# Softmax times values: two rows of probabilities in one 4-byte word, values stationary over 512 columns

## The chip, the cores and the metric

One core of a Trainium2 chip. The metric is the device time of one execution in microseconds (us), median of several. A profile's span is some 1.8 us shorter than the time of the same execution (1088.4 against 1090.23 us before), because it goes from the first to the last instruction. A profile shows one execution, so a time read off a trace is that of one execution too.

## The reference

```python
# scores: (8, 12, 1024, 1024) fp32, v: (8, 12, 1024, 64) fp32
attn = np.exp(scores - scores_max)
attn = attn / (np.sum(attn, axis=-1, keepdims=True) + 1e-8)
return np.matmul(attn, v)
```

There are 96 heads. For each, 4 MiB of scores and 256 KiB of values come in and 256 KiB go out. Both kernels leave out the maximum (the scores are standard normal) and get the row sum from a column of ones beside the values (M = 65).

## The kernel before

A partition holds 8 rows of scores (R = 8). ACT makes two rows of fp16 probabilities at a time, PE transposes each row in eight blocks of 128 x 128, DVE copies the eight blocks out of PSUM, and eight accumulating products have the transposed probabilities stationary and 65 columns of values moving.

```python
# abridged
s_pool = ...(name="spool", bufs=AHEAD)          # AHEAD = 4 heads of scores
p_pool: bufs=6; pt_pool: bufs=5; psT_pool: bufs=5 (PSUM); psO_pool: bufs=3 (PSUM)
# ... cut
def finish(u):                                   # two rows behind the transposes
    n, r, pt, st = u
    # ... cut
    for c in range(C):
        nc.tensor.matmul(out=psO[:, g, :], lhsT=pt[:, c * P : (c + 1) * P],
                         rhs=st["vones"][:, c, :], start=(c == 0), stop=(c == C - 1))
    if g == G - 1:                               # every four rows
        nc.vector.reciprocal(out=recip[:], in_=psO[:, :, D : D + 1])
        nc.vector.tensor_tensor(...)             # divide into out_sb
    if r == R - 1:
        queue(nc.sync.dma_start(out=out_bh[n], in_=st["out_sb"][:]))
# ... cut
def load(n):
    queue(nc.sync.dma_start(out=v_sb[:], in_=v_bh[n]))
    step = EB if n == BH - 1 else R              # only the last head comes in pieces of two rows
    for r in range(0, R, step):
        queue(nc.sync.dma_start(out=s_nat[:, r : r + step, :], in_=sc_bh[n, :, r : r + step, :]))
# ... cut
for r in range(R):
    if r % EB == 0:
        nc.scalar.activation(out=p_nat[:], in_=s_nat[:, r : r + EB, :], func=EXP)
    for c in range(C):
        nc.tensor.transpose(out=psT[:, c * P : (c + 1) * P], in_=p_row[:, c, :], identity=ident16[:])
    nc.vector.tensor_copy(out=pt[:], in_=psT[:])
    if r == R - 1 and n + AHEAD < BH:
        load(n + AHEAD)
    # ... cut: finish() of the row two before
```

`queue` keeps all loads and stores in program order on one queue.

The softmax here doesn't subtract the row's maximum and nothing guards it: scores larger than these inputs give would overflow.

## Time and profile before

| | before |
|---|---|
| time, median (range) | 1089.68 us (1089.3 to 1089.68, 3 runs) |
| span | 1088.4 us |
| busy: PE, DVE, ACT | 72%, 58%, 65% |
| DMA queue of loads and stores | 98.5% of 16 engines, 453.00 MB |

The queue part of the page (packets, MB, share of the 16 engines): the fetches of the program's own instructions travel over the same DMA engines.

```profile
q8 instruction: 96, 1.57, 0.6%
```

The second is the granted clock, in windows of 4 us behind the landing of the last-but-one head (length, then busy us of PE, weight loads, DVE, ACT, POOL, then PEclk, DMA share, GB/s):

```profile
1066.00:1070.00 4.00, 2.02 (x18) 1.90 (x19) 1.50 (x4) 3.98 (x3) 0.62 (x1) 0.50 0.73 294
...
1074.00:1078.00 4.00, 4.00 (x88) 4.00 (x86) 3.64 (x7) 4.00 (x3) 0.00 (x0) 1.00 0.42 165
```

The mean granted clock of 0.813 is thus no steady limit but a mixture: here 0.50 behind an idle stretch of PE (3.44 us, until 1067.98), 0.64 from 1070 to 1074, and 1.00 from 1074, when PE had been busy for some 6 us.

### The profile page before, as it was taken

The page shows a single profiled execution, that of the slowest core. Times are in us where ns is not written, and L with a number is a line of the kernel's source. Part 1 is how long each engine was busy: PE and PEld are TensorE (multiplying, and loading weights), DVE is VectorE, ACT ScalarE, POOL GpSimd, SP SyncE. Part 2 cuts the span into 40 slices and gives each one's busy share as a digit, 9 for nine tenths or more (in the row PEclk, how much of TensorE's full clock was granted, in tenths as well). Part 3 has the DMA queues.
Part 4 walks back from the last instruction along what each step waited for, and adds up shares of the span by engine and source line. Part 5 has one row for each costly group of instructions (what it writes and reads, how often), then busy time and mean ns, then how long its engine had stood idle before and what let it go on. Part 6 is the DMA issues. An engine that isn't in the chain of part 4 may idle for free.

```text
span 1088.4 us, 27687 instructions
## 1 busy us (share of the span) xinstructions
PE 782.8 (72%) x12288; PEld 743.7 (68%) x12288; DVE 628.2 (58%) x1156; ACT 704.0 (65%) x385; POOL 60.1 (6%) x102
## 2 busy tenths in 40 slices
PE   3767777676777767677776767777676777767676
PEld 3667667676766767677676767677676767767676
DVE  2556556565555655556565655655565565556555
ACT  4667576666757666665766666575665757566675
POOL 0000000000000000000000000000000000000000
PEclk9888878778787877878888887878888787787888
DMA  9999999999999999999999999999999999999994
GB/s 396 423 430 425 423 423 427 427 426 428 427 422 423 424 431 427 422 426 424 431 425 429 425 426 424 425 429 428 424 423 430 424 426 427 428 420 428 426 398 160
DMA packets 42024, 454.77 MB, mean 418 GB/s; under 512 B 4656, under 2 KB 4656, under 8 KB 29232
## 3 DMA queue, kind: packets, MB, share of 16 engines
q1 hardware_dynamic: 41904, 453.00, 98.5%
q8 instruction: 96, 1.57, 0.6%
q14 instruction: 24, 0.20, 0.0%
HBM read 427.82 MB, written 25.17 MB: 416 GB/s over the span
## 4 chain that ended last, share of the span: by engine, by line
DMA 96%; DVE 1%; PE 1%; issue 0%; SPq 0%; ACT 0%; DVEq 0%; ACTq 0%
DMA out_dram<-out_sb 69%; DMA s_nat<-in_scores_dram 18%; DMA v_sb<-in_v_dram 9%; DVE out_sb L89 1%; PE psT L140 1%; PE psO L77 0%; SPq L120 0%; ACT p_nat L136 0%; DVE pt L146 0%; SPq L115 0%; DVE recip L88 0%; DVEq L89 0%; SPq L96 0%; ACTq L136 0%
## 5 line engine op out<-in xcount | busy, mean ns | idle before, releaser
L136 ACT ACTIVATE p_nat<-s_nat 128x2048 f16<-128x2048 f32 x384 | 702.8, 1901 | 375.8 <-DMA s_nat<-in_scores_dram 364.7
L140 PE MATMUL psT<-ident,p_nat 128*128 128x128 f16 x6144 | 621.6, 264 | 274.5 <-ACT p_nat L136 273.5
L140 PEld LDWEIGHTS <-p_nat 128*128 128x128 f16 x6144 | 524.9, 155 | 301.5 <-ACT p_nat L136 295.2
L146 DVE COPY pt<-psT 128x1024 f16<-128x1024 f16 x768 | 529.0, 691 | 307.2 <-PE psT L140 285.4
L77 PE MATMUL psO<-vones,pt 128*128 128x65 f16 x6144 | 343.0, 204 | 27.3 <-DVE pt L146 26.3
L77 PEld LDWEIGHTS <-pt 128*128 128x128 f16 x6144 | 295.4, 107 | 39.2 <-DVE pt L146 38.3
L89 DVE TENSOR_TENSOR out_sb<-psO,recip 128x256 f32<-128x256 f32 x192 | 73.6, 420 | 98.7 <-DMA out_dram<-out_sb 98.6
L130 POOL CAST vones<-v_sb 128x512 f16<-128x512 f32 x96 | 59.4, 619 | 1007.3 <-DMA v_sb<-in_v_dram 995.5
L88 DVE RECIPROCAL recip<-psO 128x4 f32<-128x4 f32 x192 | 34.1, 178 | 49.9 <-PE psO L77 49.9
L136 ACT ACT_TABLE_LOAD x1 | 1.3, 1283 | 0.7 <-PEq L168 0.7
L64 DVE MEMSET vones<- 128x8 f16 x3 | 0.1, 65 | 0.8 <-PEq L168 0.8
L58 DVE CAST ident<-ident 128x128 f16<-128x128 f32 x1 | 0.2, 227 | 0.4 <-POOL ident masks.py:199 0.4
masks.py:199 POOL TENSOR_SCALAR_AFFINE_SELECT ident<-ident 128x128 f32<-128x128 f32 x1 | 0.3, 294 | 0.1
masks.py:197 POOL MEMSET ident<- 128x128 f32 x1 | 0.2, 205 | 0.3 <-POOLq L168 0.3
L168 POOL MEMSET const-float32-0.0<- 128x1 f32 x1 | 0.1, 99 | 0.2 <-issue 0.2
L168 POOL MEMSET const-bfloat16-1.0<- 128x1 bf16 x1 | 0.1, 102 | 0.0
L168 POOL MEMSET const-uint8-127<- 128x1 uint8 x1 | 0.1, 102 | 0.0
L168 POOL MEMSET const-float32-1.0<- 128x1 f32 x1 | 0.1, 99 | 0.0
## 6 DMA issues: line engine op xcount, KB each, us to landing
s_nat<-in_scores_dram SPq DMA_DIRECT2D x95, 4096.0 KB, 32.5
v_sb<-in_v_dram SPq DMA_DIRECT2D x96, 256.0 KB, 23.5
out_dram<-out_sb SPq DMA_DIRECT2D x96, 256.0 KB, 32.4
s_nat<-in_scores_dram SPq DMA_DIRECT2D x4, 1024.0 KB, 23.8
```

The lines of the kernel that those rows point to most:

```text
L58: nc.vector.tensor_copy(out=ident16[:], in_=ident32[:])
L64: nc.vector.memset(vo[:, :, D : D + 1], 1.0)
L77: nc.tensor.matmul(out=psO[:, g, :], lhsT=pt[:, c * P : (c + 1) * P], rhs=st["vones"][:, c, :], start=(c == 0), stop=(c == C - 1),)
L88: nc.vector.reciprocal(out=recip[:], in_=psO[:, :, D : D + 1])
L89: nc.vector.tensor_tensor(out=st["out_sb"][:, r - G + 1 : r + 1, :], in0=psO[:, :, 0:D], in1=recip[:].to_broadcast([P, G, D]), op=mybir.Al ...
L130: nc.gpsimd.tensor_copy(out=vones[:, :, 0:D], in_=v_sb[:])
L136: nc.scalar.activation(out=p_nat[:], in_=s_nat[:, r : r + EB, :], func=EXP)
L140: nc.tensor.transpose(out=psT[:, c * P : (c + 1) * P], in_=p_row[:, c, :], identity=ident16[:],)
L146: nc.vector.tensor_copy(out=pt[:], in_=psT[:])
L168: nc = _bacc.Bacc("TRN2", target_bir_lowering=False, num_devices=1)
```

## The change

Its intent is less work on PE. The probabilities of two rows lie side by side as two halves of a 4-byte word, so one fp32 transpose moves two rows: 32 transposes a head instead of 64. Then the values are stationary (65 columns) and four rows, 512 columns, move: 16 products a head instead of 64. The product comes out with the 65 sums on the partitions, so it is copied to SBUF and turned back by 8 small fp32 transposes.

```diff
-    p_nat = p_pool.tile([P, EB, SK], FP16)
-    nc.scalar.activation(out=p_nat[:], in_=s_nat[:, r : r + EB, :], func=EXP)
+    p_nat = p_pool.tile([P, nr // 2, SK, 2], FP16)      # the two rows are innermost
+    for q in range(nr // 2):
+        nc.scalar.activation(out=p_nat[:, q, :, :].rearrange("p j t -> p t j"),
+                             in_=s_nat[:, r0 + 2 * q : r0 + 2 * q + 2, :], func=EXP)
 ... cut
+    words = p_nat[:].rearrange("p q j t -> p q (j t)").bitcast(FP32).rearrange("p q (j c) -> p q c j", c=C)
+    for c in range(cb):
+        for q in range(nq):
+            nc.tensor.transpose(out=psT[:, c, q, :], in_=words[:, q, c0 + c, :], identity=ident[:])
+    nc.vector.tensor_copy(out=pt[:], in_=psT[:])        # 512 fp32 words
 ... cut
+    for c in range(C):
+        cols = pts[c // cb][:].rearrange("p c q i -> p c (q i)").bitcast(FP16)
+        nc.tensor.matmul(out=psO[:], lhsT=st["vones"][:, c, :], rhs=cols[:, c % cb, :],
+                         start=(c == 0), stop=(c == C - 1))
+    nc.vector.tensor_copy(out=outT[:]..., in_=psO[:])   # 65 x 512 fp32
 ... cut: emit(), one step later
+    for r in range(nr):
+        nc.tensor.transpose(out=psX[:, r, :], in_=outT[:, r // 2, :, r % 2], identity=ident[0:M, 0:M])
```

Work now goes in units of four rows (two for the last head), and a unit's result leaves two units later. So a head's store is queued behind one more load than before. The buffers change to match (probabilities 3 x 8 KiB a partition, transposed 7 tiles, PSUM 4 + 2 + 2 tiles).

More of the change, by code (lines that the diff above doesn't have):

```diff
@@ L28 @@
     BH = B * H
-    assert SQ % P == 0 and SK % P == 0
+    assert SQ % (4 * P) == 0 and SK % (2 * P) == 0
     R = SQ // P
@@ L32 @@
     M = D + 1
-    EB = 2
-    G = 4
-    LAG = 2
+    U = 4
+    TU = 512 // P
+    CB = TU * 2 // U
+    AHEAD = 4
     NV = 3
-    AHEAD = 4
     sc_bh = scores.rearrange("b h (p r) j -> (b h) p r j", p=P)
@@ L46 @@
     s_pool = ctx.enter_context(tc.tile_pool(name="spool", bufs=AHEAD))
-    p_pool = ctx.enter_context(tc.tile_pool(name="ppool", bufs=6))
+    p_pool = ctx.enter_context(tc.tile_pool(name="ppool", bufs=3))
     v_pool = ctx.enter_context(tc.tile_pool(name="vpool", bufs=AHEAD))
-    pt_pool = ctx.enter_context(tc.tile_pool(name="ptpool", bufs=5))
+    pt_pool = ctx.enter_context(tc.tile_pool(name="ptpool", bufs=7))
+    ot_pool = ctx.enter_context(tc.tile_pool(name="otpool", bufs=2))
     ob_pool = ctx.enter_context(tc.tile_pool(name="obpool", bufs=3))
     rc_pool = ctx.enter_context(tc.tile_pool(name="rcpool", bufs=4))
-    psT_pool = ctx.enter_context(tc.tile_pool(name="psTp", bufs=5, space=bass.MemoryType.PSUM))
-    psO_pool = ctx.enter_context(tc.tile_pool(name="psOp", bufs=3, space=bass.MemoryType.PSUM))
-    ident32 = const_pool.tile([P, P], FP32, name="ident32")
-    make_identity(nc, ident32)
-    ident16 = const_pool.tile([P, P], FP16, name="ident16")
-    nc.vector.tensor_copy(out=ident16[:], in_=ident32[:])
+    psT_pool = ctx.enter_context(tc.tile_pool(name="psTp", bufs=4, space=bass.MemoryType.PSUM))
+    psO_pool = ctx.enter_context(tc.tile_pool(name="psOp", bufs=2, space=bass.MemoryType.PSUM))
+    psX_pool = ctx.enter_context(tc.tile_pool(name="psXp", bufs=2, space=bass.MemoryType.PSUM))
+    ident = const_pool.tile([P, P], FP32, name="ident")
+    make_identity(nc, ident)
     vones_bufs = []
@@ L65 @@
         vones_bufs.append(vo)
-    pending = []
-    def finish(u):
-        n, r, pt, st = u
-        g = r % G
-        if g == 0:
-            st["psO"] = psO_pool.tile([P, G, M], FP32, tag="psO", name="psO")
-        psO = st["psO"]
-        for c in range(C):
-            nc.tensor.matmul(
-                out=psO[:, g, :],
-                lhsT=pt[:, c * P : (c + 1) * P],
-                rhs=st["vones"][:, c, :],
-                start=(c == 0),
-                stop=(c == C - 1),
-            )
-        if g == G - 1:
-            if r == G - 1:
-                st["out_sb"] = ob_pool.tile([P, R, D], FP32, tag="out_sb", name="out_sb")
-            recip = rc_pool.tile([P, G, 1], FP32, tag="recip", name="recip")
-            nc.vector.reciprocal(out=recip[:], in_=psO[:, :, D : D + 1])
-            nc.vector.tensor_tensor(
-                out=st["out_sb"][:, r - G + 1 : r + 1, :],
-                in0=psO[:, :, 0:D],
-                in1=recip[:].to_broadcast([P, G, D]),
-                op=mybir.AluOpType.mult,
-            )
-        if r == R - 1:
-            queue(nc.sync.dma_start(out=out_bh[n], in_=st["out_sb"][:]))
     queued = []
@@ L116, in load @@
         s_nat = s_pool.tile([P, R, SK], FP32, tag="s_nat", name="s_nat")
-        step = EB if n == BH - 1 else R
+        step = 2 if n == BH - 1 else R
         for r in range(0, R, step):
@@ L122, in load, with probs, transposed @@
         loaded[n] = (s_nat, v_sb)
+    def probs(s_nat, r0, nr):
+        p_nat = p_pool.tile([P, nr // 2, SK, 2], FP16, tag="p_nat", name="p_nat")
+        for q in range(nr // 2):
+            nc.scalar.activation(
+                out=p_nat[:, q, :, :].rearrange("p j t -> p t j"),
+                in_=s_nat[:, r0 + 2 * q : r0 + 2 * q + 2, :],
+                func=EXP,
+            )
+        return p_nat
+    def transposed(p_nat, nr):
+        words = (
+            p_nat[:]
+            .rearrange("p q j t -> p q (j t)")
+            .bitcast(FP32)
+            .rearrange("p q (j c) -> p q c j", c=C)
+        )
+        nq = nr // 2
+        cb = TU // nq
+        pts = []
+        for c0 in range(0, C, cb):
+            psT = psT_pool.tile([P, cb, nq, P], FP32, tag="psT", name="psT")
+            for c in range(cb):
+                for q in range(nq):
+                    nc.tensor.transpose(
+                        out=psT[:, c, q, :], in_=words[:, q, c0 + c, :], identity=ident[:]
+                    )
+            pt = pt_pool.tile([P, cb, nq, P], FP32, tag="pt", name="pt")
+            nc.vector.tensor_copy(out=pt[:], in_=psT[:])
+            pts.append(pt)
+        return pts
@@ new lines, in product @@
+    def product(u):
+        n, r0, nr, pts, st = u
+        nq = nr // 2
+        cb = TU // nq
+        N = nr * P
+        psO = psO_pool.tile([M, N], FP32, tag="psO", name="psO")
+        for c in range(C):
+            cols = pts[c // cb][:].rearrange("p c q i -> p c (q i)").bitcast(FP16)
+            nc.tensor.matmul(
+                out=psO[:],
+                lhsT=st["vones"][:, c, :],
+                rhs=cols[:, c % cb, :],
+                start=(c == 0),
+                stop=(c == C - 1),
+            )
+        outT = ot_pool.tile([M, nq, P, 2], FP32, tag="outT", name="outT")
+        nc.vector.tensor_copy(out=outT[:].rearrange("m q p t -> m (q p t)"), in_=psO[:])
+        return outT
@@ new lines, in emit @@
+    def emit(u, outT):
+        n, r0, nr, pts, st = u
+        psX = psX_pool.tile([P, nr, M], FP32, tag="psX", name="psX")
+        for r in range(nr):
+            nc.tensor.transpose(
+                out=psX[:, r, :], in_=outT[:, r // 2, :, r % 2], identity=ident[0:M, 0:M]
+            )
+        recip = rc_pool.tile([P, nr, 1], FP32, tag="recip", name="recip")
+        nc.vector.reciprocal(out=recip[:], in_=psX[:, :, D : D + 1])
+        if r0 == 0:
+            st["out_sb"] = ob_pool.tile([P, R, D], FP32, tag="out_sb", name="out_sb")
+        nc.vector.tensor_tensor(
+            out=st["out_sb"][:, r0 : r0 + nr, :],
+            in0=psX[:, :, 0:D],
+            in1=recip[:].to_broadcast([P, nr, D]),
+            op=mybir.AluOpType.mult,
+        )
+        if r0 + nr == R:
+            queue(nc.sync.dma_start(out=out_bh[n], in_=st["out_sb"][:]))
@@ L124, with step @@
     for n in range(min(AHEAD, BH)):
         load(n)
+    turned = []
+    summed = []
+    def step():
+        if summed:
+            emit(*summed.pop(0))
+        if turned:
+            u = turned.pop(0)
+            summed.append((u, product(u)))
     for n in range(BH):
@@ L131 @@
         st = dict(vones=vones)
-        for r in range(R):
-            if r % EB == 0:
-                p_nat = p_pool.tile([P, EB, SK], FP16, tag="p_nat", name="p_nat")
-                nc.scalar.activation(out=p_nat[:], in_=s_nat[:, r : r + EB, :], func=EXP)
-            p_row = p_nat[:, r % EB, :].rearrange("p (q c) -> p c q", c=C)
-            psT = psT_pool.tile([P, SK], FP16, tag="psT", name="psT")
-            for c in range(C):
-                nc.tensor.transpose(
-                    out=psT[:, c * P : (c + 1) * P],
-                    in_=p_row[:, c, :],
-                    identity=ident16[:],
-                )
-            pt = pt_pool.tile([P, SK], FP16, tag="pt", name="pt")
-            nc.vector.tensor_copy(out=pt[:], in_=psT[:])
-            if r == R - 1 and n + AHEAD < BH:
-                load(n + AHEAD)
-            pending.append((n, r, pt, st))
-            if len(pending) > LAG:
-                finish(pending.pop(0))
-    while pending:
-        finish(pending.pop(0))
+        nr = 2 if n == BH - 1 else U
+        for r0 in range(0, R, nr):
+            p_nat = probs(s_nat, r0, nr)
+            pts = transposed(p_nat, nr)
+            if r0 + nr == R and n + AHEAD < BH:
+                load(n + AHEAD)
+            step()
+            turned.append((n, r0, nr, pts, st))
+    while turned or summed:
+        step()
 _INS = ['scores', 'v']
```

## The prediction

The forecast's sum: per head it came to max(DMA 11.0, ACT 7.6, PE 8.9, DVE 8.1) = 11.0 us, at the end to 3 us more, and so to a span of about 1092 and a time of 1093 us. But three of its terms stand without a reason that the traces show and are estimates: 0.69 us for a copy of 512 words (the trace has 691 ns for 1024 halves), the three cases of T (about once, twice and four times the 66 ns of an fp16 transpose) with the choice of the middle one, and the 65 ns of a turn back, for which it names no source. Rival B's size was an exponential of 3.6 us, about twice the 702.8 / 384 = 1.83 us that each took of ACT before, and some 1410 us in all, as an estimate; the 1500 us that rival A could reach had no source in the traces.

> **What bounds the kernel now.** I read the busy table of the page first, then the slices, the queues, the groups, and last the end of the chain of waits. The busy table says that no compute engine is full:
>
> ```profile
> PE 782.8 (72%) x12288; PEld 743.7 (68%) x12288; DVE 628.2 (58%) x1156; ACT 704.0 (65%) x385; POOL 60.1 (6%) x102
> ```
>
> The slices and queue lines say what is full. Each digit of the DMA line is the mean busy share of the 16 DMA engines in one fortieth of the span, and the numbers below it are the GB/s that they moved:
>
> ```profile
> DMA  9999999999999999999999999999999999999994
> GB/s 396 423 430 425 423 423 427 427 426 428 427 422 423 424 431 427 422 426 424 431 425 429 425 426 424 425 429 428 424 423 430 424 426 427 428 420 428 426 398 160
> ...
> q1 hardware_dynamic: 41904, 453.00, 98.5%
> ```
>
> The kernel moves 453.00 MB through one queue, which is busy 98.5% of the span, and the rate is flat at about 425 GB/s in every slice but the first and the last two. Per head (96 of them) that is 4.72 MB. A table of two 11.0 us stretches in the middle confirms the period; its columns are length, then busy us of PE, weight loads, DVE, ACT and POOL with instruction counts, granted clock, DMA share and GB/s:
>
> ```profile
> 500.00:511.00 11.00, 7.60 (x125) 7.22 (x124) 6.36 (x13) 7.05 (x4) 0.62 (x1) 0.78 1.01 428
> 511.00:522.00 11.00, 8.15 (x130) 7.77 (x129) 6.46 (x13) 7.31 (x5) 0.62 (x1) 0.81 1.00 422
> ```
>
> 4.72 MB at 428 GB/s are 11.0 us, and a new head's exponentials start at 505.71, 516.72 and 527.73 us in the timeline, 11.01 us apart. So every head gets 11.0 us whether the engines need them or not; the busiest, PE, uses about 8, and even that is partly pipeline overlap. The groups say who waits: each compute engine stands behind the score load.
>
> ```profile
> L136 ACT ACTIVATE p_nat<-s_nat 128x2048 f16<-128x2048 f32 x384 | 702.8, 1901 | 375.8 <-DMA s_nat<-in_scores_dram 364.7
> L140 PE MATMUL psT<-ident,p_nat 128*128 128x128 f16 x6144 | 621.6, 264 | 274.5 <-ACT p_nat L136 273.5
> L146 DVE COPY pt<-psT 128x1024 f16<-128x1024 f16 x768 | 529.0, 691 | 307.2 <-PE psT L140 285.4
> L77 PE MATMUL psO<-vones,pt 128*128 128x65 f16 x6144 | 343.0, 204 | 27.3 <-DVE pt L146 26.3
> L89 DVE TENSOR_TENSOR out_sb<-psO,recip 128x256 f32<-128x256 f32 x192 | 73.6, 420 | 98.7 <-DMA out_dram<-out_sb 98.6
> L88 DVE RECIPROCAL recip<-psO 128x4 f32<-128x4 f32 x192 | 34.1, 178 | 49.9 <-PE psO L77 49.9
> ```
>
> ACT idles 365 us for loads; PE and DVE idle behind it. The only stretch that compute sets is the end. In the chain of waits, in order of time (start, length, what):
>
> ```profile
> 1032.79 33.13 DMA s_nat<-in_scores_dram
> ...
> 1066.02 1.92 ACT p_nat L136
> ...
> 1067.98 2.87 PE psT L140 x24
> ...
> 1075.08 0.53 PE psT L140 x8
> 1075.61 0.26 PE psO L77 x8
> ```
>
> The last-but-one head lands at 1066.0 and 22.4 us remain to 1088.4. There PE steps to the end: eight transposes in 0.53 us (66 ns each) and eight value products in 0.26 us (33 ns each). After an idle stretch PE is slower: 24 transposes in 2.87 us, 120 ns each. Those spacings, not the mean record lengths of 264 and 204 ns, which overlap, are what PE costs.
>
> [...]
>
> **The change part by part**, per head.
>
> *Moved over DMA: nothing changes.* Same loads, same outputs, same queue, four score buffers as before. A store is queued after one more load than before; it only has to leave its buffer within three heads, so I count nothing for it.
>
> *ACT:* four exponentials of 2048 elements, as before, but written with a step of one word (two rows interleaved). At 1.90 us each, 7.6 us. [...] nothing in this trace lets me price the stepped write; I assume the same duration.
>
> *PE removes* 64 fp16 transposes, 64 x 66 = 4.2 us, and 64 products of 65 columns, 64 x 33 = 2.1 us: 6.3 us at the warm spacing. *It adds* 16 products over 512 columns. By columns, 65 cost 33 ns, so 512 cost 260 ns, 16 x 260 = 4.2 us: twice the old products[...]. It adds 8 small transposes back, some 65 ns each, 0.5 us. And it adds 32 fp32 word transposes of unknown duration T. Three cases, estimates: T = 66[...], 2.1 us, PE total 6.8; T = 131[...], 4.2 us, total 8.9; T = 262[...], 8.4 us, total 13.1. Against the 11.0 us of DMA the break-even is T = (11.0 - 4.7) / 32 = 197 ns. I choose 131 ns as the middle[...].
>
> *DVE:* still eight copies out of the transposes, now 512 words each, 8 x 0.69 = 5.5 us, plus two reciprocals and two multiplications as before, 2 x 0.60 = 1.2 us. Added: two copies of the 65 x 512 fp32 sums, 2 x 0.69 = 1.4 us. Total 8.1 instead of 6.7 us. Fits in 11.0.
>
> *Sum in the steady state:* max(DMA 11.0, ACT 7.6, PE 8.9, DVE 8.1) = 11.0. No change. Half as many transposes are saved on an engine that does not set the time.
>
> *The end:* the only place where compute counts. ACT needs 14.5 us for the last two heads as before. PE can't start before two exponentials are done (3.7 us), since a tile now holds four rows; two heads of 8.9 us make 17.8, so it ends 21.5 us after the landing, then about 1 us of last copy, turn, reciprocal and multiplication, and 3.2 us of store (issued at 1085.2, end at 1088.4). 25.7 against 22.4 us: 3 us more. With T = 66, ACT sets this end, and what follows it (8 transposes, copy, 8 products of 256 columns, copy, 2 turns, division, store) is about 7.3 us by the same spacings, against 7.8 before: no loss. The span thus comes to 1088.4 + 3 = about 1092, and the time, 1.3 us above the span before, to 1093.
>
> **The rivals.** *A: the fp32 transposes make PE the bound.* For it: [...]the words are four bytes, and the transposes after idle are slow even now (120 ns); the words' step in the stationary operand is 32 bytes, and stepped loads already take 155 ns in the records against 107 for contiguous ones. Against it: [...]a break-even three times the present spacing. At T = 262, 13.1 us x 96 + some 30 us of start and end = about 1290[...]. *B: the stepped fp16 write slows ACT.* [...]For it: writes of half words[...]. *C: DVE waits.* One more copy in each half head, on which the turn back waits; but each turn lies a step later, and DVE keeps 2.9 us free, so I expect only the end to feel it, 1 to 3 us. *D: a gain.* All idle time that compute could return is the end, where DMA is idle for some 17 us; removing a quarter gives 0.4%. More than 2% would need the DMA rate to rise, which nothing in the change does.
>
> **Range and chances.** A is the real danger: I give T above about 200 ns one chance in five, B one in fourteen, some other stall a few per cent. That leaves about 0.69 for within 2%, 0.29 for slower, 0.02 for faster. The lower end of the range is the shortest end I can construct, 1085; the upper has to take in a moderate PE bound, 12.5 us per head, 96 x 12.5 + 30 = 1230. I predict 1093.
>
> **What would show it.** Right: DMA slices still at 9 and 420 to 430 GB/s, a head every 11.0 us, ACT still idle for score loads, word transposes spaced under 197 ns in bursts, ACT records near 1.90 us, copies near 0.69, and any difference found after the last landing. Wrong: ACT waiting for PE (its buffers not freed), DMA digits below 9, score loads landing early and waiting; exponentials well above 1.9 us would be B, fp32 transposes spaced at 200 ns or more would be A.

## The result, and the profile after

| | before | after |
|---|---|---|
| time, median (range) | 1089.68 us (1089.3 to 1090.54, 4 runs) | 1090.15 us (1089.98 to 1090.38, 4 runs) |
| span | 1088.4 us | 1088.3 us |
| busy: PE, DVE, ACT | 72%, 58%, 65% | 81%, 64%, 84% |
| mean granted clock | 0.813 | 0.964 |

The ratio is 1.0003 with an interval of 0.9986 to 1.0021: the same. A ratio here is the mean time of one kernel's fast runs over that of the other's fast runs of the same rounds, so it is not quite the ratio of the medians quoted.

The page after, first the busy table, then the slices and queues:

```profile
PE 876.8 (81%) x5392; PEld 659.4 (61%) x5392; DVE 701.6 (64%) x1353; ACT 917.4 (84%) x385; POOL 59.9 (6%) x102
...
DMA  9999999999999999999999999999999999999992
GB/s 395 426 429 425 433 427 427 426 424 434 423 430 423 431 426 429 422 429 430 427 426 426 428 426 431 426 427 429 427 429 424 425 427 431 425 427 428 426 398 81
...
q1 hardware_dynamic: 41904, 453.00, 98.3%
q8 instruction: 43, 0.70, 0.3%
```

DMA is as full as before (98.3% against 98.5% on q1), and its rate is the same to within 1% (a difference that matters below). But the compute engines all got busier, not only ACT. The groups show where:

```profile
L97 ACT ACTIVATE p_nat<-s_nat 128x2048 f16<-128x2048 f32 x384 | 916.1, 2486 | 160.7 <-DMA s_nat<-in_scores_dram 138.4
L123 DVE COPY pt<-psT 128x512 f32<-128x512 f32 x768 | 479.4, 684 | 254.8 <-PE psT L119 254.8
L119 PE MATMUL psT<-ident,p_nat 128*128 128x128 f32 x3072 | 503.7, 296 | 104.4 <-ACT p_nat L97 104.0
```

The exponentials take 2.49 us instead of 1.90 for the same count and shape (records in a row overlap a little, so four need 9.55 us of ACT and not 9.96). The copies of 512 words take 0.684 us, to within 1% what 1024 halves took (0.691). A middle window beside those in the prediction:

```profile
500.00:511.00 11.00, 8.80 (x57) 6.54 (x57) 7.28 (x14) 9.55 (x4) 0.62 (x1) 1.00 1.01 429
```

Per head ACT is at 9.55 us instead of 7.05 to 7.31, DVE at 7.28 instead of about 6.4, PE at 8.80 instead of about 7.9, the last at full clock instead of 0.78 to 0.81. The head still comes every 11.0 us.

The equal spans hide two differences at the end. In the timeline of ACT (start, length, ..., count, and the idle time before with what ended it), the last two heads' eight exponentials, before:

```profile
1066.02 14.54 ACT L136 ACTIVATE p_nat<-s_nat 128x2048 f16<-128x2048 f32 x8 [4.24 <-DMA s_nat<-in_scores_dram]
```

and after:

```profile
1059.88 19.00 ACT L97 ACTIVATE p_nat<-s_nat 128x2048 f16<-128x2048 f32 x8 [1.53 <-DMA s_nat<-in_scores_dram]
```

The last-but-one head lands 6.1 us earlier after the change, the eight exponentials take 4.5 us longer, and what follows them (to 1088.3 against 1088.4) takes 9.4 us instead of 7.8, 1.6 longer. The sum is zero to within 0.1 us. So there are three things to test: whether DMA alone hides the rest, what slows the exponential, and why the loads are done sooner.

### The profile page after: what moved, and what is told of

It reads as the page before. It is cut to its first block, busy times and chain, and to the rows that moved or that the text cites. A ratio compares the mean times of both kernels' runs of the same rounds, so it can differ in the third digit from the quotient of the medians.

```text
span 1088.3 us, 14461 instructions
## 1 busy us (share of the span) xinstructions
PE 876.8 (81%) x5392; PEld 659.4 (61%) x5392; DVE 701.6 (64%) x1353; ACT 917.4 (84%) x385; POOL 59.9 (6%) x102
## 3 DMA queue, kind: packets, MB, share of 16 engines
q1 hardware_dynamic: 41904, 453.00, 98.3%
## 4 chain that ended last, share of the span: by engine, by line
DMA 59%; ACT 20%; PE 15%; issue 4%; DVE 2%; ACTq 0%; SPq 0%
DMA s_nat<-in_scores_dram 33%; DMA out_dram<-out_sb 25%; ACT p_nat L97 20%; PE psT L119 7%; PE psO L135 7%; DVE outT L143 1%; DVE out_sb L157 1%; PE psX L150 1%; ACTq L219 0%; DVE pt L123 0%; SPq L84 0%; SPq L89 0%; ACTq L97 0%; DVE recip L154 0%
## 5 line engine op out<-in xcount | busy, mean ns | idle before, releaser
L97 ACT ACTIVATE p_nat<-s_nat 128x2048 f16<-128x2048 f32 x384 | 916.1, 2486 | 160.7 <-DMA s_nat<-in_scores_dram 138.4
L123 DVE COPY pt<-psT 128x512 f32<-128x512 f32 x768 | 479.4, 684 | 254.8 <-PE psT L119 254.8
L119 PE MATMUL psT<-ident,p_nat 128*128 128x128 f32 x3072 | 503.7, 296 | 104.4 <-ACT p_nat L97 104.0
L119 PEld LDWEIGHTS psT<-ident,p_nat 128*128 128x128 f32 x3072 | 416.4, 196 | 183.5 <-ACT p_nat L97 142.4
L135 PE MATMUL psO<-pt,vones 128*65 128x512 f16 (+1 forms) x1552 | 415.4, 386 | 0.2
L135 PEld LDWEIGHTS <-vones 128*65 128x65 f16 x1552 | 184.3, 119 | 92.8 <-issue 9.0
L150 PE MATMUL psX<-ident,outT 65*128 65x65 f32 x768 | 123.3, 283 | 103.2 <-DVE out_sb L157 99.9
L150 PEld LDWEIGHTS psX<-ident,outT 65*128 65x128 f32 x768 | 107.0, 212 | 148.8 <-DVE out_sb L157 143.3
L143 DVE COPY outT<-psO 65x512 f32<-65x512 f32 (+1 forms) x194 | 131.0, 676 | 17.0 <-PE psO L135 8.7
L157 DVE TENSOR_TENSOR out_sb<-psX,recip 128x256 f32<-128x256 f32 (+1 forms) x194 | 71.8, 407 | 0.3
```

The lines of the kernel that those rows point to most:

```text
L97: nc.scalar.activation(out=p_nat[:, q, :, :].rearrange("p j t -> p t j"), in_=s_nat[:, r0 + 2 * q : r0 + 2 * q + 2, :], func=EXP,)
L119: nc.tensor.transpose(out=psT[:, c, q, :], in_=words[:, q, c0 + c, :], identity=ident[:])
L135: nc.tensor.matmul(out=psO[:], lhsT=st["vones"][:, c, :], rhs=cols[:, c % cb, :], start=(c == 0), stop=(c == C - 1),)
L143: nc.vector.tensor_copy(out=outT[:].rearrange("m q p t -> m (q p t)"), in_=psO[:])
L150: nc.tensor.transpose(out=psX[:, r, :], in_=outT[:, r // 2, :, r % 2], identity=ident[0:M, 0:M])
L157: nc.vector.tensor_tensor(out=st["out_sb"][:, r0 : r0 + nr, :], in0=psX[:, :, 0:D], in1=recip[:].to_broadcast([P, nr, D]), op=mybir.AluOpT ...
```

## The experiments

Theory 1: DMA sets the period of both kernels, and the change costs compute time, which DMA hides. Rival: the change saves compute time and DMA hides the gain; or compute sets the period after all.

**The compute alone, before and after.** Scores are loaded for four heads only and used again for the other 92. The result is wrong; every compute instruction stays.

```diff
+        if n < AHEAD:
             s_nat = s_pool.tile([P, R, SK], FP32)
             ...load it...
+            kept.append(s_nat)
+        s_nat = kept[n % AHEAD]
```

The kernel before, so cut:

> The kernel before, with scores loaded for the first four heads only and used again for the other 92 (the result is wrong on purpose; all compute is as before, DMA falls from 453 MB to about 67 MB). Theory 1 (DMA sets the time of both kernels): well below 1089 us. By what each engine needs per head, ACT 4 x 1.83 = 7.3 us, PE 6.3 us if warm and about 8 with its stalls, DVE 6.7: about 7.5 to 8.3 us per head, 740 to 820 us. Rival (compute already sets the period of the kernel before, the DMA queue only follows it): 1040 us or more.

The changed kernel, so cut:

> The changed kernel with the same cut of the loads. Theory 1a (the change saves compute and DMA hides it): below the same cut of the kernel before, about 720 to 780 us. Theory 1b (the change costs compute, because its exponential takes 2.49 instead of 1.90 us, and DMA hides that): ACT 4 x 2.39 = 9.56 us per head, 96 x 9.56 + about 25 = 940 us, slower than the cut kernel before by 15% or more. I expect 1b.

Measured: 726.28 us for the kernel before, cut, and 936.92 us for the changed one, cut (ratios 0.6662 and 0.8594, both against the full kernel before); the first is faster than the range expected, the second as expected. DMA sets both: without it they fall by a third and by a seventh. And with DMA out of the way the change makes the kernel 29% slower (936.92 / 726.28 = 1.290). The busy table of the cut kernel before, and its timeline where PE runs without a pause at full clock (1.00 granted from 400 to 408 us, in this kernel and in the cut changed one):

```profile
PE 689.0 (95%) x12288; PEld 641.8 (89%) x12288; DVE 588.5 (81%) x1156; ACT 694.2 (96%) x385; POOL 60.1 (8%) x102
```

```profile
400.79 1.21 PE L144 MATMUL psT<-ident,p_nat 128*128 128x128 f16 x16
...
403.72 0.79 PE L77 MATMUL psO<-vones,pt 128*128 128x65 f16 x16
```

The same two views of the cut changed kernel:

```profile
PE 813.0 (87%) x5392; PEld 615.2 (66%) x5392; DVE 723.8 (77%) x1353; ACT 908.5 (97%) x385; POOL 59.9 (6%) x102
```

```profile
401.25 1.95 PE L123 MATMUL psT<-ident,p_nat 128*128 128x128 f32 x15 [0.51 <-ACT p_nat L101]
...
403.03 0.59 PE L154 MATMUL psX<-ident,outT 65*128 65x65 f32 x4
...
403.45 1.89 PE L139 MATMUL psO<-pt,vones 128*65 128x512 f16 x8
```

ACT bounds the cut changed kernel at 97%. What PE needs for one operation at full clock can be estimated by taking the mean length of one record off a burst and dividing by the other records: an fp16 transpose (1.21 - 0.23) / 15 = 65 ns, a word transpose (1.95 - 0.28) / 14 = 119 ns; a product of 65 columns (0.79 - 0.19) / 15 = 40 ns, of 512 columns (1.89 - 0.38) / 7 = 216 ns; a turn back (0.59 - 0.27) / 3 = 107 ns. Per head:

| PE us per head | before | after |
|---|---|---|
| transposes | 64 x 0.065 = 4.2 | 32 x 0.119 = 3.8 |
| products | 64 x 0.040 = 2.6 | 16 x 0.216 = 3.5 |
| turning back | | 8 x 0.107 = 0.9 |
| sum | 6.8 | 8.2 |

Half as many transposes, each at nearly twice the price, save 0.4 us; the product with only 65 stationary columns and the turning back give 1.8 us away. The first rival's gain in compute does not exist.

**What slows the exponential.** The word is made of two adjacent keys of one row instead of two rows of one key. ACT then writes contiguously; the count of every instruction stays; the moving columns of the product are read with a step of two halves, and the sums to be turned back lie contiguously too (not shown in the cut below).

```diff
-        p_nat = p_pool.tile([P, nr // 2, SK, 2], FP16)
+        p_nat = p_pool.tile([P, nr, SK], FP16)
-                out=p_nat[:, q, :, :].rearrange("p j t -> p t j"),
+                out=p_nat[:, 2 * q : 2 * q + 2, :],
 ...
-            .rearrange("p q (j c) -> p q c j", c=C)
+            .rearrange("p r (j c) -> p r c j", c=C // 2)
 ...
-                rhs=cols[:, c % cb, :],
+                rhs=cols[:, w % cb, c % 2, :],      # w = c // 2; key 2w + c % 2
```

> The changed kernel with the word made of two adjacent keys of one row instead of two rows of one key: ACT then writes without a step, the transposes stay 32 per head, and the product reads its moving columns with a step of two halves. The result stays right. If the stepped write is what slows ACT, the exponentials fall from 2.49 to 1.90 us and ACT from 9.56 to 7.3 us per head; the period stays 11.0 us (DMA) and only the end can gain, 2 to 4 us, so 1086 to 1088. If the slower exponential comes from something else, they stay near 2.49 us and the time at 1090. A stepped moving operand at half rate would show as products of 430 ns spacing instead of 216, PE 12 us per head and a time of about 1200.

Measured: correct, 1086.63 us against 1090.44 for the kernel before on that chip, ratio 0.9966 (0.9953 to 0.9978). The group of the exponentials, and their end in ACT's timeline:

```profile
L97 ACT ACTIVATE p_nat<-s_nat 128x2048 f16<-128x2048 f32 x384 | 702.0, 1899 | 369.9 <-DMA s_nat<-in_scores_dram 354.0
```

```profile
1059.42 14.51 ACT L97 ACTIVATE p_nat<-s_nat 128x2048 f16<-128x2048 f32 x8 [3.71 <-DMA s_nat<-in_scores_dram]
```

The exponential is back at 1.90 us, so the stepped write is what costs 0.59 us each (one step, of two halves, was tried). The last eight take 14.5 us again, the early landing stays, and the span is 1084.3 us (of an execution of 1086.08), 4.0 less than after the change: 0.5 from the landing and 4.5 from the exponentials, less 1.0 in the tail. The stepped moving columns cost little: in the next run 8 products take 1.97 us, against 1.89 in the cut changed kernel.

The same with the cut of the loads:

> Adjacent keys in a word, with the cut of the loads as in the two runs above (wrong result on purpose). If ACT's step is the bound of the changed kernel's compute, taking it away leaves PE: in the changed kernel PE is busy 8.8 us per head at the full clock, so 96 x 8.8 + 25 = 870 us at most, and perhaps 800 with back-to-back work, below the 940 expected of the changed kernel. If PE's work, not ACT's, were the bound there, no change against it.

Measured: 795.64 us. Without the stepped write 141 us of the change's 211 us of extra compute are gone (936.92 - 795.64 against 936.92 - 726.28); the rest is PE, which is now the bound. Not all of the gain is the exponential's: four small transposes back, now read without a step, take 0.41 us instead of 0.59 in these two cut kernels, by estimate 96 x 2 x 0.18 = 35 us of PE's time.

```profile
PE 769.4 (97%) x5392; PEld 604.9 (76%) x5392; DVE 706.1 (89%) x1353; ACT 711.3 (90%) x385; POOL 60.0 (8%) x102
```

**Why the loads are done sooner.** Theory S: the store's later place in the queue. Theory I: fewer instruction fetches over the same DMA engines. First the place of the store alone, in the kernel before:

```diff
-            queue(nc.sync.dma_start(out=out_bh[n], in_=st["out_sb"][:]))
+            stores.append((n, st["out_sb"]))     # queued after the next head's load()
```

> The kernel before, with each head's store queued one head later, behind the next load, which is where the changed kernel has it; nothing else is different. The last-but-one head landed at 1066.0 us before and at 1059.9 us after the change. Theory S (the place of the store in the queue brings the landing forward): it lands at about 1060 here too, and the end, 22.4 us later in this kernel, falls to 1083 to 1085 (time 1084 to 1086). Theory I (the landing is earlier because the changed kernel fetches fewer instructions over the same DMA engines, 43 packets instead of 96, and it has the same number here as before): it lands at 1066 within 1 us and the time stays at 1090 within 1.

Measured: 1089.95 us against 1089.98, ratio 1.0001. In its timeline:

```profile
1064.48 14.53 ACT L141 ACTIVATE p_nat<-s_nat 128x2048 f16<-128x2048 f32 x8 [4.21 <-DMA s_nat<-in_scores_dram]
```

The landing moves by 1.5 us of the 6.1 and the time not at all, so S explains a quarter of the landing at most. Theory I alone had said within 1 us of 1066, which it misses too. Then more instructions in the changed kernel, on an engine that is idle 94% of the span:

```diff
         nc.gpsimd.tensor_copy(out=vones[:, :, 0:D], in_=v_sb[:])
+        for _ in range(80):
+            nc.gpsimd.memset(dot[:], 0.0)
```

> The changed kernel with 80 tiny memsets per head added on GpSimd, which is idle 94% of the time: 7,680 more instructions to fetch, no more work for the others. Theory I (instruction fetches hold the loads up): some 30 more packets of about 16 KB; by the 6 us that 53 packets fewer seem to have brought, the last-but-one head lands 3 us later, at about 1063, and the time rises by about 3 us to 1093. Theory S: the landing stays at 1059.9 within 1 and the time at 1090.

Measured: 1648.64 us, and the experiment failed. The copies of the values, for which the products wait, stood among the memsets in GpSimd's timeline, and these took more than their records say: 138 of them fill 21.57 us between two copies, 156 ns each, against 99 ns in the records. From the groups:

```profile
L185 POOL MEMSET dot<- 128x1 f32 x7680 | 760.8, 99 | 439.5
L135 PE MATMUL psO<-pt,vones 128*65 128x512 f16 (+1 forms) x1552 | 497.7, 437 | 542.1 <-POOL dot L185 541.9
```

PE waits 542 us for the memsets, so "no more work for the others" was false, and the run says nothing of the landing. Its additional fetches also came on another queue (q14: 87 instead of 27, with 0.71 MB instead of 0.22; the 30 packets of 16 KB expected were an estimate) and left q8 at 43. The count of q8 matches PE's instructions: 12,288 products and transposes and as many weight loads, over 256, are 96 before; 2 x 5,392 / 256 are 42 after, where the page has 43. Next, each half of the change alone. Word transposes with the product as before (stationary operand read with a step of two halves):

```diff
-                lhsT=st["vones"][:, c, :], rhs=cols[:, c % cb, :],          # one per c, 512 columns
+                lhsT=cols[:, c % cb, r // 2, r % 2, :], rhs=st["vones"][:, c, :],   # per r and c
```

> One half of the change alone: two rows' probabilities in a word, 32 fp32 transposes per head, but the product as in the kernel before (64 products of 65 columns, their stationary operand now read with a step of two halves, and no turning back). From the changed kernel: exponentials 2.49 us, transposes 120 ns apart. PE 32 x 0.12 + 64 x 0.033 = 6.0 us if the stepped stationary operand costs nothing, 8 us if it makes each product 66 ns. DMA sets the period all the same, 11.0 us, and the time is 1088 to 1095. Landing of the last-but-one head: theory I with about 72 instruction packets 1063, theory S about 1060.

And fp16 transposes and contiguous exponentials as before, with stationary values and the turning back:

```diff
-            words = ...bitcast(FP32)...; nc.tensor.transpose(out=psT[:, c, q, :], ..., identity=ident[:])
+            nc.tensor.transpose(out=psT[:, c, r, :], in_=cols[:, r, c0 + c, :], identity=ident16[:])
```

> The other half alone: 64 fp16 transposes per head and contiguous exponentials as in the kernel before, values stationary over 512 columns, the sums copied and turned back. Exponentials 1.90 us; PE 64 x 0.066 + 16 x 0.216 + 8 x 0.1 = 8.5 us per head, DVE 8.1 us, under the 11.0 of DMA; time 1085 to 1092. Landing of the last-but-one head: theory I with about 66 instruction packets 1062.5, theory S about 1060.

Measured: words only 1088.60 us, ratio 0.9991 (0.9978 to 1.0005), exponentials 2.49 us, landing at 1059.97; values only 1087.88 us, ratio 0.9984 (0.9969 to 1.0), exponentials 1.90 us, landing at 1060.29. The queue lines and the last eight exponentials, words only first:

```profile
q8 instruction: 72, 1.18, 0.4%
1059.97 19.07 ACT L95 ACTIVATE p_nat<-s_nat 128x2048 f16<-128x2048 f32 x8 [1.45 <-PE psT L117]
```

```profile
q8 instruction: 66, 1.08, 0.4%
1060.29 14.53 ACT L98 ACTIVATE p_nat<-s_nat 128x2048 f16<-128x2048 f32 x8 [3.68 <-DMA s_nat<-in_scores_dram]
```

Either half alone is hidden too. They fetch 72 and 66 times, yet land as early as the changed kernel with its 43: theory I in the simple form that I had given it, so many microseconds for each fetch, falls. Both have the store in its late place and land where theory S had said, but the late store alone moved the landing by 1.5 us: neither theory accounts for it by itself.

What the landing differs by is a rate. From the first exponential to the landing of the last-but-one head, before and after (columns as in the windows above):

```profile
13.55:1066.02 1052.47, 767.70 (x12032) 729.20 (x12032) 614.33 (x1126) 688.23 (x377) 58.15 (x94) 0.81 1.01 424
14.50:1059.88 1045.38, 855.35 (x5245) 642.50 (x5246) 681.73 (x1305) 897.14 (x376) 57.97 (x94) 0.96 1.01 427
```

The DMA engines are full in both, but before they moved 446.55 MB in this stretch and after 446.10 MB: the rate after is higher by 0.6%, which is about 6 us of the 7.1 by which its stretch is shorter. By the queue lines the fetches themselves held the 16 engines for 0.6% of the span before and 0.3% after: by estimate 3 us, half of the 6.1.

A closer look at the kernel before shows when it loses the time. GpSimd copies the values of each head as they come, so its timeline is a clock of the heads:

```profile
640.69 0.62 POOL L130 CAST vones<-v_sb 128x512 f16<-128x512 f32 x1 [10.39 <-DMA v_sb<-in_v_dram]
653.08 0.62 POOL L130 CAST vones<-v_sb 128x512 f16<-128x512 f32 x1 [11.76 <-PE psT L140]
664.00 0.62 POOL L130 CAST vones<-v_sb 128x512 f16<-128x512 f32 x1 [10.31 <-DMA v_sb<-in_v_dram]
```

Most heads are 11.0 us apart, but here one is 12.39. By the same starts, gaps of 12.3 us or more come 11 times before (the expectation below says 12), every seventh to ninth head, and 8 times with words only, every tenth or eleventh. With one fetch per head before (96 for 96 heads) and 0.75 with words only, both are about eight fetches. One fetch on q8 is 1.57 MB / 96 = 16.4 KB, for 256 of PE's instructions by the counts above; why the gaps should come every eight fetches no run here shows. A late head is not idle time of DMA: in one of them, from 560.76 to 573.06, it moved 5.20 MB instead of a head's 4.72, at 423 GB/s. So the last experiment adds fetches to the kernel before, this time on PE, which has room: 32 products of one column a head, overwritten by the real product.

```diff
         psO = st["psO"]
+        for _ in range(4):
+            nc.tensor.matmul(out=psO[:, g, 0:1], lhsT=ident16[:], rhs=ident16[:, 0:1], start=True, stop=True)
```

> The kernel before with 32 one-column products added per head (64 more PE instructions, overwritten by the real product, so the result stays right); PE has 3 us per head free. In the kernel before, a head comes 1.3 us late at every eighth or ninth head, 12 times in all, with 96 instruction fetches; with 72 fetches (words only) at every tenth or eleventh, 8 times: each time about eight fetches. Theory I (every eighth instruction fetch holds a load up): here about 120 fetches, so a late head at every sixth to seventh, 14 or 15 of them, the last-but-one head lands 3 to 5 us later than 1066.0, and the time rises to 1092 to 1096. Rival (the late heads have another cause, such as the bytes loaded): still every eighth to ninth head, landing at 1066 within 1 us, and a time of 1090 to 1092 from the few extra PE us at the end alone.

Measured: correct, 1095.06 us against 1089.89, ratio 1.0051 (1.0037 to 1.0065). The queue line and the end of ACT's timeline:

```profile
q8 instruction: 120, 1.97, 0.7%
```

```profile
1070.11 14.53 ACT L140 ACTIVATE p_nat<-s_nat 128x2048 f16<-128x2048 f32 x8 [4.26 <-DMA s_nat<-in_scores_dram]
```

Gaps of 12.3 us or more now come 14 times, every sixth or seventh head, and the landing is 4.1 us later; the other 1.1 us of the 5.2 lie in the end, where the added products take PE time. PE is not full in between (82 us of 100 in a middle window), and the heads between the late ones still come 11.0 us apart. More work on PE is not it either: the run with values only keeps PE as busy (81% in both) and lands 9.8 us earlier. So the late heads go with the count of PE's instructions, about one for each eight to nine fetches (120 / 14, 96 / 11 and 72 / 8), and the rate up to the landing falls to 423 GB/s. What is shown is that more PE instructions delay the loads; of the 4.1 us the fetches' own 0.1% of the span, by estimate 1 us, is a part, and how the rest comes about is open. That the changed kernel's earlier landing comes from fewer of them fits in direction but is not shown in size: with 43 fetches there are no gaps of 12.3 us, but 13 of 11.8 to 12.0, whose cause I have not tested, and from 72 fetches down the landing no longer moves.

**Shortening the end.** A whole head waits for one 4 MiB landing near the end. The scores of the last three heads come in pieces of two rows, in three kernels:

```diff
-        step = 2 if n == BH - 1 else R
+        step = 2 if n >= BH - 3 else R
```

In the changed kernel:

> The changed kernel with the scores of the last three heads loaded in pieces of two rows (the last head's already are). Theory (DMA sets everything but the end, and the end is long because a whole head of four exponentials, 9.56 us, waits for one 4 MB landing): ACT starts on pieces as they land and is through the last-but-one head when it has landed; the last piece lands at about 1070, then one exponential of 2.5 us and a tail of 9.4 us: span about 1082, time about 1083, 6 to 7 us less than the changed kernel's 1090. Rival (the end is set by DMA bytes left, not by when ACT may start): within 1.5 us of 1090.

In the kernel before:

> The kernel before with the same split of the last three heads' loads. Its loads end some 6 us later than the changed kernel's (last-but-one head 1066.0 against 1059.9), so the last piece lands at about 1076 to 1077; then 1.9 us of exponential and 7.8 us of tail: span about 1086, time 1087 to 1088, 2 to 3 us less than 1090.

With adjacent keys:

> Adjacent keys in a word (contiguous exponentials, 1086.6 us as measured) together with the split loads, the version that these runs point to. Last piece at about 1070, 1.9 us of exponential, about 9 us of tail: span 1080 to 1082, time 1081 to 1083, faster than the kernel before by 0.7 to 0.9%. If the split gives nothing on top, 1086.6.

Measured: 1089.66 us in the changed kernel (0.9993, 0.9980 to 1.0005), 1088.53 in the kernel before (0.9985, 0.9972 to 0.9998), 1084.22 with adjacent keys (0.9949, 0.9936 to 0.9963), all correct and against 1089.79. All three gain less than expected: the first is a plain miss and ends where its rival had said, the other two end 0.5 and 1.2 us above their ranges. But the first is held up by ACT, not by bytes left. ACT's timeline of the split changed kernel (an execution of 1088.05 us, the fastest of five) has one unbroken run of 16 exponentials:

```profile
1037.88 37.86 ACT L97 ACTIVATE p_nat<-s_nat 128x2048 f16<-128x2048 f32 x16 [2.48 <-DMA s_nat<-in_scores_dram]
```

It starts one head behind and needs 9.5 us of every 11.0, so it catches up by only 1.5 us a head and is done at 1075.7, 3.1 us earlier, not 6 to 7. With adjacent keys most of the last pieces are taken as they land (one waits 0.87 us for PE); two of them:

```profile
1064.09 1.91 ACT L97 ACTIVATE p_nat<-s_nat 128x2048 f16<-128x2048 f32 x1 [1.94 <-DMA s_nat<-in_scores_dram]
1066.59 1.91 ACT L97 ACTIVATE p_nat<-s_nat 128x2048 f16<-128x2048 f32 x1 [0.59 <-DMA s_nat<-in_scores_dram]
```

Even there the gain over the version without the split is about 2 us (0.9966 to 0.9949, each against the kernel before in its own rounds), and the two intervals overlap, so it is not clear of noise; in its chain of waits the stretch behind the last landing is mostly PE and DVE work (of the 6.6 us from 1072.73 to 1079.36, 4.77 are DVE and 1.45 PE). This is the fastest version found, 0.5% under the kernel before.

## Why the prediction was right or wrong

**Right: the bound.** The result, 1090.15 us, lies in the range, 3 us under the figure. The step that carried it, that DMA sets each head's 11.0 us and anything below that is hidden, is shown by cutting the loads: 726 and 937 us.

**Wrong: the price of the exponential.** "I assume the same duration" was the mis-sized term: 2.49 us instead of 1.90, 9.55 us per head instead of 7.6. Rival B, at 3.6 us (about twice the 702.8 / 384 = 1.83 us that each took of ACT before), had the right cause and too large a size. The prediction escaped because 9.55 is still under 11.0, a margin that it had not counted on.

**PE: the sum right, by terms that partly offset.** T was 119 ns against the 131 chosen and 65 for fp16, nearest to the middle case (why, no run shows); products of 512 columns 216 ns instead of 260; the turning back 107 ns instead of 65. The old products, read as 33 ns off one stretch of the chain, took 40 in a burst, so what is removed was also a little more than the 6.3 us predicted. The sum was 8.2 us (8.80 busy) against 8.9. Rival A did not happen. The closing sentence of that sum, "Half as many transposes are saved on an engine that does not set the time", hid what its own terms said: PE's work grows, by 1.4 us a head as measured.

**DVE: somewhat too high.** 7.28 us per head against 8.1; the copy's 0.68 us was as predicted. Rival C, 1 to 3 us at the end for DVE's added copy, was not separated from the rest of the tail.

**The end: right in sum, not in its terms.** I predicted 3 us lost to PE. In fact the exponentials lost 4.5 and the tail 1.6, and an earlier landing, which I had not foreseen ("I count nothing for it" was said of the store), gave 6.1 back. That the three cancel to 0.1 us is luck.

**Rival D** (no gain over 2%) held; the best version built on the change gains 0.5%. Its argument was too strict: the DMA rate did rise a little, from 424 to 427 GB/s, though it was said that nothing in the change does that.

**Two readings** of the page were not exact. One slice in the flat stretch before has 420 GB/s, so the range is 420 to 431, where a passage had 422 to 431. And not every compute engine stands behind the score load: DVE's division (L89) waits 98.6 us in all for an output buffer, that is, for a store in the same queue. Neither changes the bound.

## What to carry to other kernels

Before work is moved off an engine, ask of the profile who sets the period; where the DMA line is 9 throughout, cut the loads in an experiment and see what the compute is worth by itself, since a change that looks free may have made it 29% dearer. Count operations with their new prices: half as many transposes of twice the width saved a tenth of their time, and the layout that allowed them made each exponential 31% longer. If a packing can be chosen, try the one that leaves the producer's writes contiguous and lets PE read with the step: here eight products then took 1.97 us instead of 1.89, and an exponential 1.90 instead of 2.49.
